# Attention in a streaming encoder step: late gates in another order, and the output weights fetched in three groups

## The chip, the cores and the metric

The kernel runs on one core of a Trainium2 chip. The core has a matrix engine (TensorE, PE in the profile), a vector engine (DVE), a scalar engine (ACT), a general engine (POOL) and a sync engine (SP). SP computes nothing; it issues the DMA transfers of its own queue, in the order of its program. The metric is device time in microseconds for one execution of the whole program, as the median of several runs.

## The reference

The program is one inference step of a two-layer encoder on 2048 prompt tokens and 32 sampled tokens, 1024 wide. Layer A is a gated DeltaNet. Layer B, with which the change is concerned, is attention over a sliding window of whole chunks of 64 tokens, with 16 query heads on 4 shared key and value heads, a learned sink per head, a gate, an output projection and a layer norm:

```python
def swa_layer(x, k, v, pos, cached, w_in, sinks, w_out, ln_g, ln_b):
    b, l, _ = x.shape
    proj = x @ w_in
    q = rope_partial(proj[..., :B_QW].reshape(b, l, B_Q_HEADS, B_HD), pos) * (B_HD ** -0.5)
    q = q.reshape(b, l, B_KV_HEADS, B_GROUP, B_HD)
    z = proj[..., B_QW:]
    sk = sinks.reshape(B_KV_HEADS, B_GROUP)
    o = cached_attention(q, k, v, sk) if cached else banded_attention(q, k, v, sk)
    out = (o * jax.nn.silu(z)) @ w_out
    return layer_norm(DN_ALPHA * x + out, ln_g, ln_b)
```

`z` is the gate. `x @ w_in` for the columns of `z` is what the text calls the gates; `@ w_out` is the output product.

## The kernel before

Every product with a weight matrix is made from two halves of each float32 factor, a high part and the rest, in three matmuls: high by high, high by low, low by high (`project`, L79 to L81). A weight slab of 128 columns is fetched whole (512 KB, `fetch_weights`, L48, into the one buffer `w_raw`), cast to its high part on ACT and subtracted on another engine (`split_fetched`, L55 and L56). The pool of slabs has two buffers, so two slabs can be used at a time.

The tokens stand in five blocks of 416 (0 to 4). The class `P2` keeps all five blocks in on-chip memory as high and low parts: blocks 0 and 1 in the pool `p2_resr` on the right side of the memory, blocks 2, 3 and 4 on the left. It makes keys, values, queries and gates. There are eight gate slabs, 0 to 7. Slabs 0 to 3 are done for all blocks; slabs 4 to 7 at first for blocks 2, 3 and 4 only. What is left, four slabs by blocks 0 and 1, are the eight late gates. They are run within attention, as work for TensorE while the first softmaxes are made. Each gate is 24 matmuls, a tanh and a scaling on ACT (L1428, L1429, tiles `zs` and `za`), one operation on DVE (L1430) and a store to `s_bz` on SP (L1431). The pool of `za` has three buffers, so the fourth gate from here writes into the buffer whose store must have landed.

`Attention.run` writes out the order of the work by hand for all five engines. It takes the chunks 14 to 31 and then 0 to 13, in steps: scores, largest value, exponentials, shares, transposes (L1713), values (L1731), and the gating of the result. Between the first steps `fill(n)` lets the generator `gates` go on by n half gates: two gates before the first exponentials, one each in the three places after them, and one in each of the steps 0, 1 and 2. The gates' sums use the two banks `oa` and `ob` in turn, the same two that hold the values' result of each step.

From step 3 on, each step has one half of an output product (512 of 1024 columns, eight weights, each with three matmuls, L1146 to L1148). The output weights lie split in memory as `s_wob`; weight k takes 1 MB with both parts. `weights` (L1468) fetches weights 0 to 2 in the course of the third late gate. `load_late` (L1484) fetches 3 to 7: its pool needs the memory of `P2`'s right side, which is free when the last late gate is done, in step 2. Behind the first two of these five SP asks for the first row tile `r` (L1547), and behind the rest for the layer norm's tables and for the keys and values of the chunks 0 to 11.

Two lines show how the late gates are placed before the change:

```python
for j, i in enumerate((6, 7, 4, 5)):
    for b in (0, 1):
```

The slabs 6 and 7 are still in the two buffers; 4 and 5 are fetched and split a second time, 4 in the course of the third gate and 5 in the course of the fifth.

Of the kernel before, what the change touches and what calls it, by code (L numbers as in the profile page):

```python
# [11 lines left out]
F32 = mybir.dt.float32  # L12
# [9 lines left out]
D = 1024  # L22
# [70 lines left out]
def drain(gen):  # L93
    for _ in gen:
        pass


class P1:
# [243 lines left out]
    def split(self):  # L342
        self.cast()
        self.subtract()
# [947 lines left out]
class P2:  # L1292
# [3 lines left out]
    def __init__(self, tc, right, spare, I, O, T):  # L1296
        self.tc, self.nc, self.I, self.O, self.T = tc, tc.nc, I, O, T
        self.resr = new_pool(tc, right, "p2_resr", 1, side="right")
        self.wp = new_pool(tc, right, "p2_w", 2, side="right")
        self.wk = new_pool(tc, right, "p2_wk", 3, side="right")  # L1300
        self.stg = new_pool(tc, spare, "p2_stg", 2, side="right")
        self.ppr = new_pool(tc, spare, "p2_psr", 2, PSUM, side="right")
        self.ppl = None
        self.turn = 0
        self.x = {}
        self.w = {}

    def load_right(self):
        for b in (0, 1):
            self.load(b, self.resr)  # L1310

    def open_left(self, left):
        self.resl = new_pool(self.tc, left, "p2_resl", 1, side="left")
# [120 lines left out]
class Attention:  # L1434


    EARLY = 3

    def __init__(self, tc, left, I, O, T, G):
        self.tc, self.nc, self.I, self.O, self.T, self.G = tc, tc.nc, I, O, T, G  # L1440
        nc, V = tc.nc, tc.nc.vector
        L = "left"
        self.one = one = new_pool(tc, left, "t_one", 1, side=L)
        self.two = new_pool(tc, left, "t_two", 3, side=L)
        self.thr = new_pool(tc, left, "t_thr", 4, side=L)
# [12 lines left out]
        self.sinks = one.tile([128, 12, 2], F32, tag="twice", name="twice")  # L1458
        V.tensor_copy(self.sinks[:], raw[:].unsqueeze(2).to_broadcast([128, 12, 2]))
        self.S = [self.ps_s.tile([128, 2, 2, 256], F32, tag=f"S{p}", name="S") for p in range(2)]  # L1460
        self.held = {}
# [9 lines left out]
    def load_early(self):  # L1471
        self.w = self.weights(self.first, 0, self.EARLY)

    def open_right(self, right):
        tc, I = self.tc, self.I
# [2 lines left out]
        self.otwo = new_pool(tc, right, "u_two", 2, side=R)  # L1478

    def load_late(self):  # L1480
        w = self.oone.tile([128, 2, KC - self.EARLY, D], F32R, tag="wo", name="wo")
        for k in range(self.EARLY, KC):
            x = w[:, :, k - self.EARLY]
            self.nc.sync.dma_start(x.bitcast(F32), self.T["wob"][:, k].rearrange("a p d -> p a d"))  # L1484
            self.w.append(x)
            if k == self.EARLY + 1:
                yield
# [456 lines left out]
def program(tc, I, O, T, G):  # L1944
# [99 lines left out]
    att = Attention(tc, left, I, O, T, G)  # L2044

    def gates(raw):
        for j, i in enumerate((6, 7, 4, 5)):
            for b in (0, 1):
                g = p2.gate(i, (b,), lambda: att.out_bank(b))
                next(g)  # L2050
                next(g)
                if b == 0:
                    if j in (1, 2):
                        p2.w[3 + j] = split_fetched(nc, p2.wp, raw, nc.vector)
                    if j == 1:
                        raw = fetch_weights(nc, p2.wp, I["b_w_in"][13])
                    if j == 1:
                        att.load_keys(18, 32)
                        att.load_values(18, 32)
                        att.load_early()  # L2060
                yield
                drain(g)
                yield

    def opened():
        right.close()
# [164 lines left out]
```

## Time and profile before

| what | value |
|---|---|
| median of 3 runs | 2122.08 us (2119.59 to 2124.72) |
| the profiled execution's own time | 2119.22 us |
| its span | 2117.1 us |
| TensorE busy | 2078.8 us, 98% |
| VectorE, ScalarE, GpSimd busy | 62%, 43%, 39% |
| mean DMA rate | 145 GB/s |
| late gates and first steps of attention | about 1719 to 1784 us |
| first output product | from 1783.76 us |

The span is the time from the first to the last instruction of the program in one profiled execution; all times within it count from its start. TensorE is busy nearly all the time, so time is lost where it waits, and where it is granted half its clock. The views used below are the list of waits (who waited for whom: total, times, longest), the chain of waits, the timeline of an engine (start, length, engine, line, what, and in brackets the idle time before and what ended it) and windows (busy time of PE, its weight loads, DVE, ACT and POOL with their counts, then the granted clock, the mean share of the DMA engines, and GB/s).

### The profile page before, as it was taken

The page shows a single profiled execution, that of the slowest core. Times are in us where ns is not written, and L with a number is a line of the kernel's source. Part 1 is how long each engine was busy: PE and PEld are TensorE (multiplying, and loading weights), DVE is VectorE, ACT ScalarE, POOL GpSimd, SP SyncE. Part 2 cuts the span into 40 slices and gives each one's busy share as a digit, 9 for nine tenths or more (in the row PEclk, how much of TensorE's full clock was granted, in tenths as well). Part 3 has the DMA queues.
Part 4 walks back from the last instruction along what each step waited for, and adds up shares of the span by engine and source line. Part 5 has one row for each costly group of instructions (what it writes and reads, how often), then busy time and mean ns, then how long its engine had stood idle before and what let it go on. Part 6 is the DMA issues. An engine that isn't in the chain of part 4 may idle for free.

```text
span 2117.1 us, 37205 instructions
## 1 busy us (share of the span) xinstructions
PE 2078.8 (98%) x14062; PEld 1912.6 (90%) x14062; DVE 1306.6 (62%) x2449; ACT 901.1 (43%) x2263; POOL 834.6 (39%) x1179
## 2 busy tenths in 40 slices
PE   8999999999999999999999999999999998999998
PEld 6999999999999999999888888999999996777775
DVE  4676666666557688889978885225543223566665
ACT  4444444445622377677752212322111233455552
POOL 1422222222122187878830302136443103566765
PEclk9999999999999999999999999999999998999999
DMA  5222332346664545556846764455222257534321
GB/s 206 67 65 82 111 111 92 96 128 207 197 197 153 178 157 180 163 171 210 278 159 204 240 194 131 135 196 202 82 72 70 75 143 259 137 100 120 100 72 65
DMA packets 263636, 307.26 MB, mean 145 GB/s; under 512 B 71409, under 2 KB 194609, under 8 KB 263185
## 3 DMA queue, kind: packets, MB, share of 16 engines
q1 hardware_dynamic: 252208, 281.40, 42.7%
q10 hardware_dynamic: 11248, 23.48, 3.4%
q8 instruction: 111, 1.82, 0.4%
q14 instruction: 69, 0.56, 0.1%
HBM read 188.58 MB, written 116.60 MB: 144 GB/s over the span
## 4 chain that ended last, share of the span: by engine, by line
PE 91%; POOL 3%; DMA 2%; DVE 2%; ACT 1%; issue 1%; SPq 1%; ACTq 0%; POOLq 0%; DVEq 0%
PE ps L79 17%; PE ps L81 17%; PE ps L80 17%; PE ot L1146 3%; PE po L1146 3%; PE po L1148 3%; PE po L1147 3%; PE ot L1148 3%; PE ot L1147 3%; PE S L1698 2%; PE ot L1731 2%; PE tr L1713 2%; POOL tm L729 1%; POOL Tt L731 1%; PE g L695 1%; PE gq L831 1%
## 5 line engine op out<-in xcount | busy, mean ns | idle before, releaser
L79 PE MATMUL ps<-act_hi,w_hi 128*128 128x416 f32 x1936 | 683.3, 354 | 1.4 <-ACT act_hi L70 1.4
L81 PE MATMUL ps<-act_hi,w_lo 128*128 128x416 f32 x1936 | 681.3, 352 | 0.9 <-POOL w_lo L56 0.9
L80 PE MATMUL ps<-act_lo,w_hi 128*128 128x416 f32 x1936 | 678.2, 350 | 0.4 <-DVE act_lo L71 0.4
L79 PEld LDWEIGHTS ps<-act_hi,w_hi 128*128 128x128 f32 x1936 | 364.1, 188 | 6.6 <-ACT act_hi L70 2.1
L80 PEld LDWEIGHTS ps<-act_lo,w_hi 128*128 128x128 f32 x1936 | 363.8, 188 | 4.8 <-DVE act_lo L71 0.8
L81 PEld LDWEIGHTS ps<-act_hi,w_lo 128*128 128x128 f32 x1936 | 363.4, 188 | 4.7 <-POOL w_lo L56 1.3
L56 POOL TENSOR_TENSOR w_lo<-w_raw,w_hi 128x1024 fp32r<-128x1024 f32 x44 | 117.1, 2661 | 470.3 <-ACT w_hi L55 443.1
L209 DVE SCALAR_TENSOR_TENSOR y<-R,convw,y 128x2083 f32<-128x2083 f32 x72 | 182.7, 2538 | 62.8 <-ACT y L206 46.9
L1537 POOL TENSOR_TENSOR P<-e,sm 128x384 f32<-128x384 f32 (+2 forms) x128 | 101.2, 812 | 181.7 <-DVE sm L1527 175.7
L729 POOL TENSOR_TENSOR tm<-L,Tt 128x60 f32<-128x60 f32 (+19 forms) x365 | 133.2, 365 | 78.8 <-issue 39.9
L731 POOL TENSOR_TENSOR Tt<-Tt,tm 128x60 f32<-128x60 f32 (+19 forms) x365 | 140.8, 386 | 28.6
L1523 ACT ACTIVATE e<-S,nm 128x193 f32<-128x193 f32 (+2 forms) x260 | 104.8, 416 | 95.9 <-DVE nm L1518 58.2
L1146 PE MATMUL ot<-wo,g_hi 128*128 128x512 f32 x256 | 104.6, 409 | 6.1 <-DMA wo<-s_wob 6.1
L305 ACT COPY R<-ps 128x416 f32<-128x416 f32 (+1 forms) x144 | 60.3, 442 | 108.3 <-PE ps L81 95.7
L1146 PE MATMUL po<-wo_hi,g_hi 128*128 128x512 f32 x256 | 103.3, 404 | 0.2 <-ACT g_hi L1188 0.2
L1345 POOL TENSOR_TENSOR rs<-rs,sin 128x416 f32<-128x416 f32 x50 | 70.7, 1414 | 80.3 <-DVE rs L1344 73.5
L1148 PE MATMUL ot<-wo,g_lo 128*128 128x512 f32 x256 | 101.2, 395 | 0.0
L1147 PE MATMUL ot<-wo,g_hi 128*128 128x512 f32 x256 | 101.1, 395 | 0.0
L1148 PE MATMUL po<-wo_hi,g_lo 128*128 128x512 f32 x256 | 100.2, 392 | 0.5 <-DVE g_lo L1189 0.5
L1430 DVE SCALAR_TENSOR_TENSOR za<-zs,za 128x416 f32<-128x416 f32 x40 | 31.7, 796 | 111.3 <-ACT za L1429 111.1
L1147 PE MATMUL po<-wo_lo,g_hi 128*128 128x512 f32 x256 | 99.9, 390 | 0.0
L55 ACT CAST w_hi<-w_raw 128x1024 fp32r<-128x1024 f32 x46 | 48.3, 1051 | 93.5 <-PE ps L80 74.4
(299 smaller groups left out, 3917.9 us busy)
## 6 DMA issues: line engine op xcount, KB each, us to landing
w_raw<-in_w_in SPq DMA_DIRECT2D x40, 512.0 KB
w_raw<-in_b_w_in SPq DMA_DIRECT2D x18, 512.0 KB
k<-s_k SPq DMA_DIRECT2D x17, 512.0 KB
E<-s_E SPq DMA_DIRECT2D x17, 512.0 KB
s_bz<-za SPq DMA_DIRECT2D x40, 208.0 KB
s_bq<-ra SPq DMA_DIRECT2D x40, 208.0 KB
s_q<-y SPq DMA_DIRECT2D x8, 1024.0 KB
s_wo<-wo_parts SPq DMA_DIRECT2D x16, 512.0 KB
```

Source lines behind the costliest of these rows:

```text
L56: sub.tensor_tensor(out=lo[:], in0=raw[:], in1=hi[:], op=ALU.subtract)
L79: nc.tensor.matmul(ps, hi[:, k, :], xh[:, k, :], start=(k == 0), stop=False)
L80: nc.tensor.matmul(ps, hi[:, k, :], xl[:, k, :], start=False, stop=False)
L81: nc.tensor.matmul(ps, lo[:, k, :], xh[:, k, :], start=False, stop=(k == KC - 1))
L209: nc.vector.scalar_tensor_tensor(out=y[:], in0=R[:, j:j + W], scalar=self.convw[:, i, j:j + 1], in1=y[:], op0=ALU.mult, op1=ALU.add)
L729: P.tensor_tensor(out=tm[:n, i0 - k:, :w], in0=L[:n, i0:, j:j + 1].to_broadcast(sh), in1=Tt[:n, j:j + 1, :w].to_broadcast(sh), op=ALU.mult)
L731: P.tensor_tensor(out=Tt[:n, i0:, :w], in0=Tt[:n, i0:, :w], in1=tm[:n, i0 - k:, :w], op=ALU.subtract)
L1146: nc.tensor.matmul(ps[:n], ghi[:, k, :n], hi, start=a, stop=False)
L1147: nc.tensor.matmul(ps[:n], ghi[:, k, :n], lo, start=False, stop=False)
L1148: nc.tensor.matmul(ps[:n], glo[:, k, :n], hi, start=False, stop=z)
L1523: self.nc.scalar.activation(x.e[:, h, u, :x.n], x.S[:, h, u, :], AF.Exp, bias=x.nm[:, h, u:u + 1], scale=1.0, accum_out=x.sm[:, h, u:u + 1])
L1537: self.nc.gpsimd.tensor_tensor(out=x.P[:, u, :nj * 128].rearrange("r (j h k) -> r j h k", h=2, k=64), in0=x.e[:, :, u, :n].rearrange("r h ...
```

## The change

The eight late gates get another order, written as pairs of slab and block: (6,0), (7,0), (7,1), (4,0), (5,0), (4,1), (5,1), (6,1). Block 0 is used for the last time by the fifth of them. It now has a pool of its own, `p2_resf`, which is closed in the sixth gate, and the memory goes to a new pool on the left side for the output weights 3, 4 and 5, asked for at that point. Weights 0, 1 and 2 are asked for one in the course of the fourth gate and two in the fifth, where all three were asked for in the third. `load_late` keeps 6 and 7. Since slab 6 is used first and last, it is fetched and split once more: three slabs are split in the late gates (4 in the second gate, 5 ahead of the fourth, 6 in the seventh) where there were two.

```diff
+        self.front = ExitStack()
+        self.resf = new_pool(tc, self.front, "p2_resf", 1, side="right")
...
         for b in (0, 1):
-            self.load(b, self.resr)
+            self.load(b, (self.resf, self.resr)[b])
...
     EARLY = 3
+    LATE = 6
...
     def weights(self, pool, a, z):
         w = pool.tile([128, 2, z - a, D], F32R, tag="wo", name="wo")
+        self.w += [w[:, :, k] for k in range(z - a)]
         for k in range(a, z):
             self.nc.sync.dma_start(w[:, :, k - a].bitcast(F32), self.T["wob"][:, k].rearrange("a p d -> p a d"))
-        return [w[:, :, k] for k in range(z - a)]
+            yield
...
+    def middle_weights(self, left):
+        return self.weights(new_pool(self.tc, left, "t_wo2", 1, side="left"), self.EARLY, self.LATE)
...
     def load_late(self):
...
+        drain(self.weights(self.oone, self.LATE, KC))
+        yield
         self.tabs = ln_tables(self.nc.sync, self.oone, self.I["b_ln_g"], self.I["b_ln_b"])
...
+        for m, (i, b) in enumerate(((6, 0), (7, 0), (7, 1), (4, 0), (5, 0), (4, 1), (5, 1), (6, 1))):
+            if m == 3:
+                split(5)
+            g = p2.gate(i, (b,), lambda: att.out_bank(m % 2))
+            next(g)
+            next(g)
+            if m == 1:
+                split(4)
+            elif m == 2:
+                att.load_keys(18, 32)
+                att.load_values(18, 32)
+                early = att.early_weights()
+            elif m == 3:
+                next(early)
+            elif m == 4:
+                drain(early)
+            elif m == 5:
+                p2.front.close()
+                drain(att.middle_weights(left))
+            elif m == 6:
+                split(6)
+            yield
+            drain(g)
+            if m in (1, 4):
+                raw = fetch_weights(nc, p2.wp, I["b_w_in"][8 + (5, 6)[m // 4]])
+            yield
```

The first place is SP's queue during the late gates, from the values of chunks 18 to 31 (`vd`) to the row tile (of the after, stores and loads for later steps are left out at the dots). `wo` are output weights of 1 MB each, `s_bz<-za` the gates' stores, `w_raw` a gate slab, `qs` and `zs` queries and gates of coming steps, `r` the row tile. Before:

```order
L1497 DMA vd<-s_bv 64x14x128 x2
L1468 DMA wo<-s_wob 128x2x1024 x3
L1431 DMA s_bz<-za 128x416 x3
L1676 DMA qs<-s_bq 128x8x64 x2
L1681 DMA zs<-s_bz 128x8x128
L1431 DMA s_bz<-za 128x416
L1676 DMA qs<-s_bq 128x8x64 x2
L1431 DMA s_bz<-za 128x416
L1681 DMA zs<-s_bz 128x8x128
L1484 DMA wo<-s_wob 128x2x1024 x2
L1547 DMA r<-s_h 128x1024
L1484 DMA wo<-s_wob 128x2x1024 x3
```

The same stretch of SP's queue in the changed kernel:

```order
L1433 DMA s_bz<-za 128x416
L1473 DMA wo<-s_wob 128x2x1024
L1433 DMA s_bz<-za 128x416
L1473 DMA wo<-s_wob 128x2x1024 x2
L1433 DMA s_bz<-za 128x416
L48 DMA w_raw<-in_b_w_in 128x1024
L1679 DMA qs<-s_bq 128x8x64 x2
L1684 DMA zs<-s_bz 128x8x128
L1473 DMA wo<-s_wob 128x2x1024 x3
L1433 DMA s_bz<-za 128x416
...
L1473 DMA wo<-s_wob 128x2x1024 x2
L1550 DMA r<-s_h 128x1024
```

The three early weights stand between the gates' stores now, three more stand behind the first queries and gates, and two are left ahead of the row tile.

The second place is ACT's queue from the first late gate's end to the first copy of a transpose (`pt`). `zs` and `za` are a gate's tanh and scaling, `e` the exponentials of one softmax, `w_hi` the cast of a gate slab. Before:

```order
L1428 ACTIVATE zs<-ot 128x416
L1429 ACTIVATE za<-ot 128x416
L1523 ACTIVATE e,sm<-S,nm 128x193 x4
L55 CAST w_hi<-w_raw 128x1024
L1428 ACTIVATE zs<-ot 128x416
L1429 ACTIVATE za<-ot 128x416
L1523 ACTIVATE e,sm<-S,nm 128x193 x4
L1428 ACTIVATE zs<-ot 128x416
L1429 ACTIVATE za<-ot 128x416
L1523 ACTIVATE e,sm<-S,nm 128x193 x4
L1719 COPY pt<-tr 128x384
L55 CAST w_hi<-w_raw 128x1024
```

In the changed kernel:

```order
L55 CAST w_hi<-w_raw 128x1024
L1430 ACTIVATE zs<-ot 128x416
L1431 ACTIVATE za<-ot 128x416
L1526 ACTIVATE e,sm<-S,nm 128x193 x4
L1430 ACTIVATE zs<-ot 128x416
L1431 ACTIVATE za<-ot 128x416
L1526 ACTIVATE e,sm<-S,nm 128x193 x4
L55 CAST w_hi<-w_raw 128x1024
L1430 ACTIVATE zs<-ot 128x416
L1431 ACTIVATE za<-ot 128x416
L1526 ACTIVATE e,sm<-S,nm 128x193 x4
L1722 COPY pt<-tr 128x384
```

The cast of slab 4 moved from behind the first exponentials to the place ahead of the second gate's tanh, and the cast of slab 5 from behind the fourth gate and the first copy to the place ahead of that gate's tanh. The subtractions on DVE moved in the same way. POOL's rows stand as they stood.

More of the change, by code (lines that the diff above doesn't have):

```diff
@@ L1466, in weights, with early_weights @@
         w = pool.tile([128, 2, z - a, D], F32R, tag="wo", name="wo")
+        self.w += [w[:, :, k] for k in range(z - a)]
         for k in range(a, z):
             self.nc.sync.dma_start(w[:, :, k - a].bitcast(F32), self.T["wob"][:, k].rearrange("a p d -> p a d"))
-        return [w[:, :, k] for k in range(z - a)]
-    def load_early(self):
-        self.w = self.weights(self.first, 0, self.EARLY)
+            yield
+    def early_weights(self):
+        return self.weights(self.first, 0, self.EARLY)
+    def middle_weights(self, left):
+        return self.weights(new_pool(self.tc, left, "t_wo2", 1, side="left"), self.EARLY, self.LATE)
     def open_right(self, right):
@@ L1480, in load_late @@
     def load_late(self):
[L1481 to L1487, printed above, removed]
+        drain(self.weights(self.oone, self.LATE, KC))
+        yield
         self.tabs = ln_tables(self.nc.sync, self.oone, self.I["b_ln_g"], self.I["b_ln_b"])
@@ L2046, in gates, with split @@
     def gates(raw):
[L2047 to L2063, printed above, removed]
+        def split(j):
+            p2.w[j] = split_fetched(nc, p2.wp, raw, nc.vector)
+        for m, (i, b) in enumerate(((6, 0), (7, 0), (7, 1), (4, 0), (5, 0), (4, 1), (5, 1), (6, 1))):
[24 more added lines that the diff above has]
+            yield
     def opened():
```

1 line of the change is left out of this document (added).

## The prediction

> **What bounds the kernel now.** I read the page, the list of waits, the timelines of TensorE (PE) and of the sync queue (SP), and windows for clock and DMA. What the change can win is idle or slow TensorE in its own stage, out of a span of 2117.1 us.
>
> ```profile
> span 2117.1 us, 37205 instructions
> ...
> L1146 PE MATMUL ot<-wo,g_hi 128*128 128x512 f32 x256 | 104.6, 409 | 6.1 <-DMA wo<-s_wob 6.1
> ```
>
> The second row is the output product of attention: its 6.1 us of idle time are waits for the output weights. The waits between 1690 and 1830 us add another, and the chain of waits says how old it is:
>
> ```profile
> ACT za L1429 <- DMA s_bz<-za: 2.8, 1, 2.8
> ...
> PE ot L1731 <- ACT za L1429: 1.8, 1, 1.8
> ```
>
> ```profile
> 1745.27 13.19 DMA s_bz<-za
> ```
>
> A gate's result leaves through one of three za buffers. The store issued at 1745.27 lands 13.19 us later, behind 3 MB of weights; ScalarE (ACT) waits 2.8 us for its buffer and TensorE 1.8 us for ACT. What both stalls cost is read from TensorE's timeline (start, length, what, idle before):
>
> ```profile
> 1740.98 0.43 PE L79 MATMUL ot<-act_hi,w_hi 128*128 128x416 f32 x1
> ...
> 1756.60 0.64 PE L1731 MATMUL ot<-pt,vd 64*64 64x256 f32 x2
> ...
> 1764.28 0.43 PE L79 MATMUL ot<-act_hi,w_hi 128*128 128x416 f32 x1
> ...
> 1770.49 1.82 PE L1731 MATMUL ot<-pt,vd 64*64 64x256 f32 x24
> ...
> 1773.72 0.43 PE L79 MATMUL ot<-act_hi,w_hi 128*128 128x416 f32 x1
> ...
> 1783.76 0.48 PE L1146 MATMUL ot<-wo,g_hi 128*128 128x512 f32 x1
> ...
> 1788.37 0.50 PE L1146 MATMUL ot<-wo,g_hi 128*128 128x512 f32 x1 [1.42 <-DMA wo<-s_wob]
> ...
> 1794.76 0.80 PE L1146 MATMUL ot<-wo,g_hi 128*128 128x512 f32 x1 [0.91 <-DMA wo<-s_wob]
> ...
> 1797.32 0.80 PE L1146 MATMUL ot<-wo,g_hi 128*128 128x512 f32 x1 [0.91 <-DMA wo<-s_wob]
> ...
> 1801.77 1.53 PE L1731 MATMUL ot<-pt,vd 64*64 64x256 f32 x24
> ...
> 1804.70 0.48 PE L1146 MATMUL ot<-wo,g_hi 128*128 128x512 f32 x1
> ...
> 1810.32 0.82 PE L1713 MATMUL tr<-ident,P 128*128 128x128 f32 x6
> 1811.06 0.92 PE L1698 MATMUL S<-kT,qs 64*128 64x192 f32 x8
> 1811.91 0.45 PE L1731 MATMUL ot<-pt,vd 64*64 64x256 f32 x4
> ```
>
> Stall A: from the values to the next gate 1756.60 to 1764.28, 7.68 us; the same work one step later, 1770.49 to 1773.72, takes 3.23. A costs 4.45. Stall B: from the first output product to the values of the next step 1783.76 to 1801.77, 18.01 us; one step later 1804.70 to 1811.91, 7.21. B costs 10.80. Both exceed the idle time because the clock falls as well (last three figures of a row: granted clock, DMA share, GB/s):
>
> ```profile
> 1757.43:1760.84 3.41, 1.71 (x20) 0.92 (x22) 1.81 (x4) 0.89 (x2) 0.96 (x2) 1.00 0.81 186
> 1760.84:1764.25 3.41, 3.41 (x22) 2.28 (x15) 0.94 (x3) 1.87 (x9) 0.66 (x1) 0.50 1.15 303
> 1784.73:1788.14 3.41, 2.22 (x10) 1.46 (x8) 1.00 (x3) 1.72 (x8) 2.03 (x3) 1.00 1.02 419
> 1788.14:1791.56 3.42, 0.97 (x3) 0.48 (x3) 0.00 (x0) 0.00 (x0) 1.21 (x2) 1.00 1.02 411
> ```
>
> TensorE busy for 1.71 of 3.41 us is followed by a stretch at 0.50; busy for 2.22 it is followed by 1.00. A gap of 1.2 us costs itself, one of 1.7 us also half of 3.41, that is 1.7 us.
>
> **The change, part by part.** I call the eight late gates G0 to G7. TensorE's work is the same 24 matmuls a gate, in another order.
>
> *Weights 3 to 7 of the output product.* Three of the five that B waited for are now asked for after G4, two where all five stood. The late request:
>
> ```profile
> 1780.55 0.93 SPq L1484 DMA_DIRECT2D wo<-s_wob  x2
> ```
>
> Two of 1 MB go out at 1780.55, call it T0; the second is there when the wait at 1788.37 ends, T0+7.8. In the changed kernel these two are the last ones, numbers 6 and 7. The product starts at T0+3.2 and takes (1810.32 - 1804.70)/8 = 0.70 us for each of eight weights, so number 7 is wanted at T0+8.1: just in time. The row of activations r comes 1.3 us later (half of the 2.56 us a megabyte takes, 1794.76 to 1797.32) and is wanted when the product ends, at T0+8.8, with 1.6 us of transposes and scores (1810.32 to 1811.91) before TensorE needs its bank again. B goes, 10.80, if the queue is empty at T0. Between the stages it was idle:
>
> ```profile
> 1765.00:1770.00 5.00, 5.00 (x32) 4.75 (x32) 1.07 (x3) 2.63 (x11) 1.62 (x2) 1.00 0.02 5
> ...
> 1775.00:1780.00 5.00, 5.00 (x35) 4.53 (x34) 1.01 (x3) 3.19 (x11) 1.62 (x2) 1.00 0.01 1
> ```
>
> That is 10 us; the change puts 3 MB and 0.5 MB of gate weights in front, 9.0 us at 2.56. It fits with 1 us to spare. What goes back on B if the cover is gone: 2.56 us for each megabyte still queued, and half clock beyond 1.2 us of gap.
>
> *Early weights 0 to 2*, now between the gates' stores. The store that took 13.19 us stands in front of them, so A goes, 4.45; za's next wait is for a store one megabyte later, with more than a gate's time in hand. The three weights land about 1 us later (two more stores of 208 KB ahead of them) and are wanted at T0+3.2: nothing.
>
> *SP's new wait.* The first middle weight waits for TensorE to leave the first block (end of G4). Behind it on SP stand G5's store, the next queries, G6's store and the next gates' loads; none is read before T0. The loads ahead of the new wait held SP long in the run before:
>
> ```profile
> 1747.76 8.21 SPq L1676 DMA_DIRECT2D qs<-s_bq  x2
> ```
>
> That holds SP until 1756, when the run before was through with its sixth gate too (the values at 1756.60 follow it), so G4 is done even 4.1 us later: nothing, and 1 us at most if SP came earlier, since only the queue's slack pays.
>
> *Gate weights w4 and w5, needed earlier.* This is the cost. Before, w4 was used by the fifth gate and w5 by the seventh; now by G3 and G4, one and two gates sooner, while w5's fetch stands where it stood:
>
> ```profile
> 1735.68 1.34 SPq L48 DMA_DIRECT2D w_raw<-in_b_w_in  x1
> ```
>
> Its landing has no row, since nobody waited. I bound it by bytes. Issued since 1722.7, up to and with it:
>
> ```profile
> qs<-s_bq SPq DMA_DIRECT2D x4, 256.0 KB
> w_raw<-in_b_w_in SPq DMA_DIRECT2D x2, 512.0 KB
> zs<-s_bz SPq DMA_DIRECT2D x2, 512.0 KB
> s_bz<-za SPq DMA_DIRECT2D x2, 208.0 KB
> kT<-s_bk SPq DMA_DIRECT2D x1, 384.0 KB
> vd<-s_bv SPq DMA_DIRECT2D x2, 192.0 KB
> ```
>
> ```profile
> 1722.70:1740.00 17.30, 17.30 (x100) 15.86 (x101) 4.99 (x8) 7.70 (x26) 1.62 (x2) 1.00 1.10 255
> ```
>
> 4256 KB are 4.36 MB; 255 GB/s for 17.3 us are 4.41 MB. It lands at 1740.0 at the earliest, and as the 16 engines end apart I take 1741.5 as the late end. Then come the cast and the subtraction:
>
> ```profile
> 1744.20 1.08 ACT L55 CAST w_hi<-w_raw 128x1024 fp32r<-128x1024 f32 x1
> ```
>
> ```profile
> 1733.61 1.23 DVE L56 TENSOR_TENSOR w_lo<-w_raw,w_hi 128x1024 fp32r<-128x1024 f32 x1 [2.79 <-ACT w_hi L55]
> ```
>
> They end at 1742.3 to 1743.8. G4 starts where the fifth gate started, 1740.98, and gets 0.4 us of work done with the high part alone. Stall C is 0.9 to 2.4 us. I take 2.4, since a transfer counts only when its slowest engine is done, and 1.7 for the clock, since a window with 2.4 us of gap is emptier than the one that halved it above: 4.1. For w4 the queue holds 1408 KB (kT, two qs, itself), a third of that, 5.7 us at 255 GB/s, so it lands between 1728.4 and about 1730; its cast now heads ACT's queue ahead of G1's tanh and the first exponentials, which come 3 us later, and the first transposes (just before 1740.98) still find their input about 1 us early: nothing, and up to 1 us if not.
>
> The Trainium skill (TensorE: Matmul & The Clock Gate, "Why this matters for your kernels") asks for no gaps above about 3 us between bursts of matmuls. By that, C would not touch the clock, and the sum below would be 1.7 us lower. The rows above, in which 1.7 us of gap in one window was enough, speak against it, and I keep 1.7.
>
> *A third split (w6 again for G7).* A cast of 1.08 and a subtraction of 1.23 us more. Their cover is the wait of ACT and VectorE (DVE) for G6's matmuls:
>
> ```profile
> 1769.09 0.52 ACT L1428 ACTIVATE zs<-ot 128x416 f32<-128x416 f32 x1 [1.29 <-PE ot L81]
> ```
>
> ```profile
> 1770.05 0.59 DVE L1430 SCALAR_TENSOR_TENSOR za<-zs,za 128x416 f32<-128x416 f32 x1 [3.98 <-ACT za L1429]
> ```
>
> 1.08 goes into 1.29: nothing, or about 1 us if the cast comes late, since the values wait for this gate's bank.
>
> *Block 0 in a pool of its own.* No work is added. It makes the planner move two fetches of gate weights behind stores, and three products behind four small steps, near 1111 to 1128 us, where TensorE is full:
>
> ```profile
> 1125.00:1130.00 5.00, 5.00 (x24) 4.14 (x23) 4.78 (x10) 1.05 (x1) 0.00 (x0) 1.00 0.92 284
> ```
>
> I take nothing, and 1 us either way since DVE has 0.22 us free there.
>
> **Sum.** -4.45 (A) - 10.80 (B) + 4.1 (C) = -11.15 us. The profiled execution took 2119.22, its span and 2.1 us around it: 2108.1. The median shown, 2122.08, is 2.9 above that execution and would give 2110.9. I forecast 2109.5, between the two.
>
> **Rivals.**
> 1. C is small: the raw w5 lands at 1740 and the clock holds. -15.25 + 0.9 = -14.3, 2105 to 2108. For it: the bytes; against it: the slowest engine. 0.19.
> 2. B goes only in part: the queue is not empty at T0, since small packets move slower than the weights (255 against 411 GB/s in the rows). With 2 MB left, 5.1 us come back and half clock for one window: -11.15 + 6.8 = -4.3, 2115 to 2118. Against it: 10 us idle for 9.0. 0.17; about half of it lies inside 0.2%.
> 3. Slower: the memory of block 0 comes free late. If SP's new wait ended only near T0 (say with G6, because the new tile also covers bytes still in use), all that stands behind it goes out there: 3 MB, three stores of 208 KB, 512 KB of queries and 512 KB of gates ahead of the last 2 MB. Before, the last weight landed at 1797.3, T0+16.7, behind 5 MB and r; now 1.1 MB more, T0+19.5, and r after it, 4.1 us in all. B is then 14.9 with A gone and C paid: +3.8, and 1.3 for w6's fetch in the same queue: +5.1, 2124 to 2127. It decides from a wait that ends 5 us before T0 or later. Against it: only one TensorE event is waited for, and the pool closes after G4. 0.06.
> 4. Nothing measurable: C cascades through ACT's queue (exponentials behind the cast of w5) until it eats A and most of B, 10 us more than I take: 2118 to 2121. No row shows such a chain, since the next transposes wait for TensorE's own gate. 0.03.
>
> **How the numbers follow.** My forecast has 0.55, from C's and the 1 us bounds 2106.5 to 2113. The range 2104 to 2119 takes in rivals 1 and 2 and leaves out 3 and 4 and the tails. 0.2%, about what a measurement of this kernel can tell from no change, is 4.2 us: faster means under 2117.8. Faster 0.55 + 0.19 + half of rival 2, rounded to 0.83; same, 0.11, from the rest of 2 and from 4; slower 0.06.
>
> **What would show it.** Right: no wait of TensorE on wo and none of za on s_bz; first product to next values near 7.2 us; one wait of G4's matmuls on ACT's w_hi and DVE's w_lo, some 2.4 us, and 0.50 clock behind it; the queue idle just before the last two weights go out. Wrong: waits on weights 6 and 7, or SP standing at the middle weights until G6.

## The result, and the profile after

The changed kernel takes 2112.1 us, the median of six runs (2111.02 to 2116.91), beside 2121.76 us for the kernel before (2119.59 to 2124.72, six runs): a ratio of 0.9964, with a 95% interval of 0.9952 to 0.9975 (the two medians by themselves give 0.9954, inside the interval). Run once more, in a later batch, it took 2111.1 us (2109.43 to 2115.35) beside 2120.0: 0.9958, 0.9944 to 0.9973. The profiled execution took 2112.2 us, its span 2110.4.

The page's row of the output product has no idle time left, where 6.1 us stood:

```profile
span 2110.4 us, 37218 instructions
...
L1146 PE MATMUL ot<-wo,g_hi 128*128 128x512 f32 x256 | 103.6, 405 | 0.0
```

The list of waits between 1690 and 1830 us names neither wo nor s_bz any more. What TensorE waits for now is the gate weights, stall C; for the row tile r only DVE waits (columns: total, times, longest, us):

```profile
ACT w_hi L55 <- DMA w_raw<-in_b_w_in: 6.3, 2, 5.5
...
DVE r L1154 <- DMA r<-s_h: 2.4, 1, 2.4
...
PE ot L79 <- ACT w_hi L55: 1.2, 1, 1.2
...
PE ot L81 <- DVE w_lo L56: 0.6, 1, 0.6
```

The timeline of TensorE after the change (start, length, what, idle before):

```profile
1730.89 0.92 PE L1701 MATMUL S<-kT,qs 64*128 64x192 f32 x8
1731.74 0.46 PE L79 MATMUL ot<-act_hi,w_hi 128*128 128x416 f32 x1
...
1745.01 0.46 PE L79 MATMUL ot<-act_hi,w_hi 128*128 128x416 f32 x1 [1.20 <-ACT w_hi L55]
...
1746.27 0.71 PE L81 MATMUL ot<-act_hi,w_lo 128*128 128x416 f32 x1 [0.61 <-DVE w_lo L56]
...
1756.83 0.43 PE L79 MATMUL ot<-act_hi,w_hi 128*128 128x416 f32 x1
...
1763.05 0.45 PE L1734 MATMUL ot<-pt,vd 64*64 64x256 f32 x4
...
1766.28 0.43 PE L79 MATMUL ot<-act_hi,w_hi 128*128 128x416 f32 x1
...
1785.76 0.48 PE L1146 MATMUL ot<-wo,g_hi 128*128 128x512 f32 x1
...
1793.16 0.66 PE L1734 MATMUL ot<-pt,vd 64*64 64x256 f32 x8
...
1796.10 0.48 PE L1146 MATMUL ot<-wo,g_hi 128*128 128x512 f32 x1
...
1803.37 0.88 PE L1734 MATMUL ot<-pt,vd 64*64 64x256 f32 x12
```

From the values to the next gate it takes 1763.05 to 1766.28, 3.23 us, so A is gone; from the first output product to the next values 1785.76 to 1793.16, 7.40 us in place of 18.01, so B is gone. C shows at 1745 and 1746 us, and half clock follows it; just ahead of T0 (1782.54 here) the transfers run out (last three figures of a row: granted clock, DMA share, GB/s):

```profile
1742.82:1746.23 3.41, 1.64 (x12) 0.94 (x8) 1.24 (x2) 2.18 (x5) 0.00 (x0) 1.00 1.10 297
1746.23:1749.65 3.42, 3.38 (x10) 3.23 (x11) 1.89 (x4) 1.90 (x9) 1.62 (x2) 0.50 1.19 193
...
1775.00:1780.00 5.00, 5.00 (x31) 4.87 (x30) 1.63 (x4) 2.96 (x14) 1.62 (x2) 1.00 0.82 211
1780.00:1782.50 2.50, 2.50 (x21) 1.69 (x19) 1.00 (x3) 1.96 (x4) 0.15 (x1) 1.00 0.05 15
```

The sync queue's timeline, with the three middle weights and, at T0, the last two:

```profile
1755.80 6.59 SPq L1684 DMA_DIRECT2D zs<-s_bz  x1
1762.48 1.85 SPq L1473 DMA_DIRECT2D wo<-s_wob  x3
...
1782.54 0.93 SPq L1473 DMA_DIRECT2D wo<-s_wob  x2
```

From here on I cut each profiled execution at two places of TensorE's timeline: the first scores (1730.89 above) and the second values after the first output product (1803.37 above). Between them lies what I call the opening, 72.5 us; behind them the rest, 307.0 us to the end of the span. The kernel before has 83.6 (1728.30 to 1811.91) and 305.2.

| kernel | opening, us | rest, us | half clock in the opening behind | ratio to the kernel before, 95% |
|---|---|---|---|---|
| before | 83.6 | 305.2 | A and B | 1 |
| changed | 72.5 | 307.0 | C | 0.9964 (0.9952 to 0.9975) |
| changed, again | 72.6 | 307.0 | C | 0.9958 (0.9944 to 0.9973) |
| five weights late again | 84.1 | 305.4 | C and B | 1.0016 (1.0007 to 1.0024) |
| early weights at once | 71.4 | 307.0 | none | 0.9971 (0.9961 to 0.9981) |
| w5's gate later | 68.6 | 307.0 | none | 0.9955 (0.9943 to 0.9967) |
| w5's gate later, early weights at once | 73.3 | 307.0 | A | single run |
| weights 32 bytes up | 71.3 | 305.2 | none | 0.9954 (0.9942 to 0.9966) |
| w5's gate later, 32 bytes up | 68.5 | 305.2 | none | 0.9948 (0.9932 to 0.9964) |
| w5's gate later, 96 bytes up | 68.9 | 306.4 | none | 0.9940 (0.9923 to 0.9957) |
| w5's gate later, 64 bytes up | 69.2 | 307.2 | none | 0.9951 (0.9932 to 0.9970) |
| high and low part side by side | 70.9 | 307.0 | none | single run |
| before, front pool alone | 81.9 | 305.5 | B | 1.0010 (0.9997 to 1.0023) |
| before, weights 96 bytes up | 81.8 | 304.6 | B | 0.9997 (0.9985 to 1.0009) |

Of the six executions with 96 bytes, one took 2553.17 us at a granted clock of 0.75 and is left out of the ratio. The medians of the kernel before differ by up to 3.4 us between batches (2118.40 to 2121.76), so a term of 1 or 2 us is read from these stages and their waits, not from the medians. Each stage comes from one profiled execution.

### The profile page after: what moved, and what is told of

Its sections match the earlier page's. It is cut to its first block, busy times and chain, and to the rows that moved or that the text cites. A ratio compares the mean times of both kernels' runs of the same rounds, so it can differ in the third digit from the quotient of the medians.

```text
span 2110.4 us, 37218 instructions
## 1 busy us (share of the span) xinstructions
PE 2076.7 (98%) x14062; PEld 1911.9 (91%) x14062; DVE 1309.2 (62%) x2450; ACT 901.9 (43%) x2264; POOL 833.9 (40%) x1179
## 4 chain that ended last, share of the span: by engine, by line
PE 92%; DVE 3%; DMA 2%; POOL 1%; ACT 1%; issue 1%; SPq 0%; ACTq 0%; DVEq 0%; POOLq 0%
PE ps L79 17%; PE ps L81 17%; PE ps L80 17%; PE ot L1146 3%; PE ot L1147 3%; PE ot L1148 3%; PE po L1146 3%; PE po L1148 3%; PE po L1147 3%; PE S L1701 2%; PE ot L1734 2%; PE tr L1716 2%; PE g L695 1%; PE gq L831 1%; PE ks L846 1%; PE sp L846 1%
```

## The experiments

### Is B the gain, and do A and C cancel?

The changed kernel with all five weights late again; gates, early weights and pool as changed:

```diff
-        drain(self.weights(self.oone, self.LATE, KC))
+        late = self.weights(self.oone, self.EARLY, KC)
+        next(late)
+        next(late)
         yield
+        drain(late)
...
-                drain(att.middle_weights(left))
```

> The changed kernel with weights 3 to 7 asked for late again, two ahead of the row tile and three behind it, as in the kernel before; gate order, three splits and spread early weights stay. Theory: the gain is stall B alone, 10.6 us by the profile after, while A (4.45 won) and C (3.9 paid) cancel; the products lose the 0.05 us they each take longer (31 of them, 1.6 us). So B returns: first product to next values 16 to 18 us, 2112.1 + 10.6 - 1.6 = about 2121 us. Rival (the gates' order and the spread stores made the gain): 2112 to 2115 us.

It took 2122.11 us (2117.88 to 2125.8) beside 2118.4: 1.0016, no gain at all. TensorE's timeline shows B as it was:

```profile
1787.22 0.48 PE L1146 MATMUL ot<-wo,g_hi 128*128 128x512 f32 x1
...
1791.88 0.50 PE L1146 MATMUL ot<-wo,g_hi 128*128 128x512 f32 x1 [1.47 <-DMA wo<-s_wob]
1795.73 0.62 PE L1146 MATMUL ot<-wo,g_hi 128*128 128x512 f32 x1 [2.88 <-DMA wo<-s_wob]
...
1805.28 1.08 PE L1737 MATMUL ot<-pt,vd 64*64 64x256 f32 x8
```

From 1787.22 to 1805.28 are 18.06 us. The waits show no za behind s_bz, and C is there (1.7 and 0.6 us of TensorE's waits). So all of the gain hangs on the three weights that go out earlier, and what the new order of gates wins by A it pays for C.

### Does spreading the early weights take A away?

First on the changed kernel, with weights 0 to 2 asked for in the third gate all at once, as before:

```diff
-                early = att.early_weights()
-            elif m == 3:
-                next(early)
-            elif m == 4:
-                drain(early)
+                drain(att.early_weights())
```

> The changed kernel with weights 0 to 2 asked for in one go in the third gate again, ahead of that gate's store. Theory that spreading them is what ended stall A: ACT waits for s_bz again and 4.45 us come back, 2116.5 us. Rival: the wait for w5 delays the sixth gate by 3.9 us, and the store, 5.1 us later than now (two more weights ahead), lands at about 1757 us after the start of the profile's span, before that gate's za is written at 1761: no wait, 2112 us within 1.

A did not come back: no wait on s_bz, 2111.96 us (2110.22 to 2117.74), opening 71.4. My reason had named the spreading, so this spoke against it. But a store still stands behind 3 MB, three at a time:

```profile
1747.02 0.64 SPq L1473 DMA_DIRECT2D wo<-s_wob  x1
1747.76 4.96 SPq L1433 DMA_DIRECT2D s_bz<-za  x3
```

The first of the three is complete at 1760.54, 12.8 us after its issue (13.19 in the kernel before), and ACT takes its buffer again at 1760.62. It was in time by 0.1 us, in an execution in which C had held back every gate by 2.8 us. So the next run asks for the weights at once where C is gone, on the kernel with w5's gate one place later (below):

```diff
-                early = att.early_weights()
-            elif m == 3:
-                next(early)
-            elif m == 4:
-                drain(early)
+                drain(att.early_weights())
+            elif m == 4:
                 split(5)
```

> The kernel with w5's gate one place later (where stall C is gone), and output weights 0 to 2 asked for all three in the third gate, as in the kernel before. With C in place such a request cost nothing: the store behind it landed at 1760.54 us and its buffer was wanted at 1760.62, so C's 2.9 us of delay may have been the cover. Theory (without C the buffer is wanted about 2.3 us earlier, so stall A comes back in part, and spreading the request is what keeps it away): ACT waits 1.5 to 2.5 us for za on s_bz, TensorE 0.5 to 1.7 us behind it; 69.3 to 70.3 us from the first score to the second values in place of 68.6, 1.7 more if a half clock follows. Rival (the order of the gates removes A whatever the request): no such wait, 68.6 us.

A is back. The waits around the opening:

```profile
ACT za L1431 <- DMA s_bz<-za: 2.6, 1, 2.6
...
PE ot L1734 <- ACT za L1431: 1.6, 1, 1.6
```

The chain of waits has the store again, with the time it took to land:

```profile
1749.43 12.56 DMA s_bz<-za
```

And in the windows half clock follows:

```profile
1760.93:1764.34 3.41, 1.72 (x21) 0.89 (x22) 1.77 (x4) 0.89 (x2) 0.92 (x2) 1.00 1.12 316
1764.34:1767.75 3.41, 3.41 (x21) 2.23 (x16) 0.98 (x3) 1.79 (x9) 0.69 (x1) 0.50 0.84 230
```

The opening is 73.3 us against 68.6 without this edit. Of these 4.7 us, 4.25 lie between the values and the next gate (1760.34 to 1767.82, 7.48 in place of 3.23), which is A, half clock included. The other 0.4 us fall at the values one step earlier; the runs with 96 and 64 bytes below, which have no such edit, lose 0.3 and 0.6 there too. So spreading the request does take A away. In the changed kernel it is only a second cover, since C's delay hides A too.

### C alone: the gate of w5 one place later

```diff
-        for m, (i, b) in enumerate(((6, 0), (7, 0), (7, 1), (4, 0), (5, 0), (4, 1), (5, 1), (6, 1))):
-            if m == 3:
-                split(5)
+        for m, (i, b) in enumerate(((6, 0), (7, 0), (7, 1), (4, 0), (4, 1), (5, 0), (5, 1), (6, 1))):
...
             elif m == 4:
                 drain(early)
-            elif m == 5:
+                split(5)
+            elif m == 6:
                 p2.front.close()
                 drain(att.middle_weights(left))
-            elif m == 6:
                 split(6)
```

> Order (6,0), (7,0), (7,1), (4,0), (4,1), (5,0), (5,1), (6,1): slab 5 is used one gate later, its split stands in the fifth gate, and the memory of block 0 goes over one gate later. Theory: C is the landing of w5's raw slab, so no wait on w_hi or w_lo remains and 3.9 us go, 2108.2 us, if the queue keeps up; in the profile after it was busy until 1782.4 and the last two weights went out at 1782.5, so with 3.9 us less time before it weight 7 and the row tile may come some 2.4 us late, 2110.6 us. Rival (C is made by the order of casts and exponentials on ACT, not by the landing): a wait of 2 us or more moves to the sixth gate, 2112 us.

The split of slab 5 and the release of block 0's memory move back with the gate. TensorE waits for no gate weights any more, and the late gates start at an even pace:

```profile
1731.82 0.46 PE L79 MATMUL ot<-act_hi,w_hi 128*128 128x416 f32 x1
...
1743.65 0.43 PE L79 MATMUL ot<-act_hi,w_hi 128*128 128x416 f32 x1
...
1753.03 0.43 PE L79 MATMUL ot<-act_hi,w_hi 128*128 128x416 f32 x1
...
1762.48 0.43 PE L79 MATMUL ot<-act_hi,w_hi 128*128 128x416 f32 x1
```

From the first late gate after the first scores to the fourth it takes 1731.82 to 1753.03, 21.2 us, where the changed kernel takes 1731.74 to 1756.83, 25.1: C costs 3.9 us. The three middle weights now go out two us later, and the first product still reaches the next values in 7.4 us. The margin is smaller, though: transfers ran at a share of 1.05 up to 1778.00, 0.75 us ahead of the last two weights (1778.75), where the changed kernel had 2.5 us with a share of 0.05; part of that slack was C's delay. The run took 2109.14 us (2107.17 to 2111.19), 0.9955: not resolved against the changed kernel by the medians, but the stage is 3.9 us shorter.

### When the half clock follows a gap

C did not cost the same everywhere. With the same two waits in TensorE's row (1.2 to 1.7 and 0.6 us), half clock followed in the changed kernel, in its repeat and with five weights late; it did not with the early weights at once, the weights 32 bytes up or the parts side by side, and there the same stage took 24.0, 24.0 and 23.5 us in place of 25.1 to 25.6. The windows below tell why. They are laid so that one begins where a half clock of the same execution begins, and follow each other by 3.413 us. The changed kernel again:

```profile
1740.39:1743.80 3.41, 1.67 (x12) 0.94 (x8) 0.94 (x1) 1.95 (x4) 0.00 (x0) 1.00 0.99 293
1743.80:1747.22 3.42, 3.08 (x9) 2.95 (x10) 2.19 (x5) 1.60 (x9) 1.62 (x2) 0.50 1.19 205
```

The early weights at once:

```profile
1742.06:1745.47 3.41, 1.79 (x16) 1.23 (x12) 0.41 (x1) 2.17 (x7) 0.00 (x0) 1.00 1.01 313
1745.47:1748.88 3.41, 2.79 (x15) 2.51 (x14) 2.71 (x5) 1.45 (x6) 1.62 (x2) 1.00 1.18 198
```

The weights 32 bytes up:

```profile
1740.64:1744.06 3.42, 1.75 (x15) 1.13 (x12) 0.47 (x1) 1.88 (x5) 0.00 (x0) 1.00 1.08 324
1744.06:1747.47 3.41, 2.79 (x16) 2.59 (x15) 2.65 (x5) 1.44 (x7) 1.62 (x2) 1.00 1.20 187
```

The first busy figure is TensorE's: 1.64, 1.67 and 1.72 us (the run with A, above) of 3.41 are followed by 0.50, 1.75 and 1.79 by 1.00. In these rows the switch lies at about half of a window. Where the windows begin is different in each execution: where C's second wait of 0.6 us falls into the next window, as in the last two, the first wait alone does not empty half of one. So a gap of 1.2 to 2.3 us costs 1.7 us more, or not, depending on where a window happens to begin. The same holds for A: the two later kernels with A in place had no half clock behind it, and there values to next gate took 5.2 (front pool alone) and 6.3 us (before, 96 bytes up) in place of 7.68. The Trainium skill (TensorE: Matmul & The Clock Gate, "What's actually happening") says that the window runs free of the kernel and lasts 3413 ns, and the runs agree: a half clock behind A or C lasts 3.41 us and begins at a different place of the work each time. It has the clock fall after an idle window, and here a half-idle one was enough.

The busy figure sorts only the windows of attention's opening. Further ahead, among smaller matmuls, it does not. In the changed kernel TensorE was busy throughout a window, and half clock followed:

```profile
735.88:739.30 3.42, 3.42 (x30) 3.04 (x30) 1.88 (x4) 2.57 (x8) 1.90 (x7) 1.00 0.45 147
739.30:742.71 3.41, 3.41 (x18) 2.82 (x16) 1.07 (x4) 3.21 (x13) 2.65 (x9) 0.50 0.51 156
```

In the kernel before, 1.58 us busy of the window at 1016.73 were followed by 1.00; in the run with A back, 1.80 us of the one at 1027.06 by 0.50. So half of a window is no rule for the whole program, and what the clock goes by stays open.

### What the output product lost: 1.8 us behind the opening

The sum of the prediction ended at the opening. Behind it the changed kernel lost 1.8 us (307.0 against 305.2), in steps whose order of work the change does not touch. The step from values to values shows it; the kernel before:

```profile
1852.53 1.53 PE L1731 MATMUL ot<-pt,vd 64*64 64x256 f32 x24
...
1862.69 1.53 PE L1731 MATMUL ot<-pt,vd 64*64 64x256 f32 x24
```

The changed kernel:

```profile
1854.40 1.53 PE L1734 MATMUL ot<-pt,vd 64*64 64x256 f32 x24
...
1864.61 1.53 PE L1734 MATMUL ot<-pt,vd 64*64 64x256 f32 x24
```

10.16 us have become 10.21. From the second product to the last, 29 steps, it is 292.86 us in place of 291.33, so 1.5 of the 1.8 us lie there; the other 0.3 fall between the start of the last product and the end, which takes 21.07 us in the kernel before, 21.41 in the changed one and 21.36 in the kernel before with the front pool alone, whose output weights lie where they lay. The product's own time I read from its weight loads (PEld): its 24 loads take 5.24 us from first to last start, 5.20 before, as medians over the products of an execution. In the kernel before, the first nine matmuls are about 234 ns apart and those with the late weights settle to 227 ns; now nearly all run at 232 to 234. What differs for them is where their operands lie in on-chip memory: weights 0 to 2 at byte 114688 of a partition in both kernels, 3 to 7 at 180192 before, now 3 to 5 at 139264 and 6 and 7 at 204768. The other factor, g_hi, moved too, from 163296 to 187872 for one of its buffers, by a multiple of 128. I took the rest of the address by 64 for the cause, and moved weights 0 to 5 by 32 bytes:

```diff
+        if a == 0:
+            pool.tile([128, 8], F32, tag="pad", name="pad")
         w = pool.tile([128, 2, z - a, D], F32R, tag="wo", name="wo")
```

> The changed kernel with output weights 0 to 5 placed 32 bytes higher in on-chip memory (at 32 instead of 0 modulo 64); nothing else moves. In the profile before, products over weights at 32 modulo 64 settle at 227 ns a matmul and those over weights at 0 modulo 64 run at 233 to 234. Theory (alignment): a product falls from 5.24 to about 5.1 us, 31 of them win 4.2 us, 2108 us. Rival (the place, left or right of the memory, or the size of the tile decides): 5.24 us stay, 2112 us.

```profile
1851.04 1.53 PE L1736 MATMUL ot<-pt,vd 64*64 64x256 f32 x24
...
1861.18 1.53 PE L1736 MATMUL ot<-pt,vd 64*64 64x256 f32 x24
```

A step takes 10.14 us, a product 5.18, the rest 305.2 us: the 1.8 us are back, but not the 4.2 that I expected: the spacing fell from 233 to 230 ns on average, not to 227. So the place of the weights alone moves a product's time, and the rule was not right. Two more sizes of the same pad, both with w5's gate later, and one of them on the kernel before:

> The kernel with w5's gate one place later, and the output weights 0 to 5 moved up by 96 bytes in place of 32, so that all of their addresses leave the same rest by 128 (96) as weights 6 and 7 and the products' other operand, g. Theory 1 (what counts is whether the two operands of a product leave the same rest by 128; O1's do, and its products run at 227 ns): 227 ns throughout, a product of 24 takes about 5.11 us in place of 5.24, 31 of them -4.0 us, what follows the second values 303 us; total about 2105. Theory 2 (only the rest by 64 counts, which the 32 bytes changed already): as with 32 bytes, 5.18 us, 305.2 us behind the second values; total 2107. Theory 3 (placement is not it): 5.24 us, 307.0, total 2109. The opening of attention stays at 68.6 us in all three.

> As the run beside it, with 64 bytes in place of 96: weights 0 to 5 leave the rest 64 by 128, and 0 by 64 as in the changed kernel. Theory 1 (same rest by 128 as g): not the same, so slow, about 5.24 us for a product of 24 matmuls and 307 us behind the second values. Theory 2 (rest by 64): 5.24 us as well. Rival (any shift helps, as neighbouring tiles no longer collide): 5.18 us or less, 305 us. Total 2109 by the theories, 2107 by the rival.

> The kernel before with nothing changed but the place of its output weights 0 to 2, 96 bytes further up, where they leave the same rest by 128 as weights 3 to 7 and g. In the kernel before, the first nine matmuls of each product come 234 ns apart and settle to 227 ns with the later weights. Theory 1: all at 227 ns, a product takes 5.11 us in place of 5.19, 31 of them -2.5 us; what follows the second values takes 302.7 us in place of 305.2; ratio 0.9988. Theory 2 (rest by 64): at least the same gain. Theory 3 (the spacing has another cause, such as what DVE or ACT do beside the first third of a product): 5.19 us, 305.2 us, ratio 1.000.

96 bytes up, the step is 10.18 us:

```profile
1850.06 1.53 PE L1736 MATMUL ot<-pt,vd 64*64 64x256 f32 x24
...
1860.24 1.53 PE L1736 MATMUL ot<-pt,vd 64*64 64x256 f32 x24
```

A product takes 5.22 us at 96 bytes, 5.23 to 5.24 at 64, and 5.17 in the kernel before moved by 96 bytes (5.20 unmoved; rest 304.6 us). Both rules fall: by 64, 32 and 96 should be alike; by 128, 96 should be the fastest. The times of these runs were 2107.73 us with 96 bytes (the median of all six), 2109.94 with 64 and 2119.38 for the kernel before moved. A last guess was the distance between the high and the low part of a weight:

```diff
-        w = pool.tile([128, 2, z - a, D], F32R, tag="wo", name="wo")
-        self.w += [w[:, :, k] for k in range(z - a)]
+        w = pool.tile([128, z - a, 2, D], F32R, tag="wo", name="wo")
+        self.w += [w[:, k] for k in range(z - a)]
...
-            self.nc.sync.dma_start(w[:, :, k - a].bitcast(F32), self.T["wob"][:, k].rearrange("a p d -> p a d"))
+            self.nc.sync.dma_start(w[:, k - a].bitcast(F32), self.T["wob"][:, k].rearrange("a p d -> p a d"))
```

> The changed kernel with another layout of the output weights alone: high and low part of one weight side by side (4096 bytes apart) in place of all high parts ahead of all low parts (12288 bytes apart for weights 0 to 5, 8192 for 6 and 7). In the kernel before, products settled to 227 ns with weights 3 to 7 (20480 apart) and in O1 (32768 apart), and ran at 232 to 234 ns with 12288 and 8192. Theory (the distance between the two parts sets the spacing): the time of a product moves off 5.24 us by at least 0.05 us, either way. Rival (distance has no part in it): 5.23 to 5.25 us. Attention's opening stays at 71.3 to 72.5 us.

One run took 2113.87 us; a product takes 5.24 us as before this edit, with the same sequence of spacings. The distance is not it. What is shown: the median product repeats to the nanosecond between runs on different chips for one placement (5.239 us in every run with the changed kernel's places, 5.181 in both with 32 bytes up), and a shift of the weights alone moves it. How much of the step from 5.20 to 5.24 us is due to the weights and how much to g_hi was not tried, and which property of the place decides stays open.

### The front pool: not nothing

O1 is the output product of layer A, long ahead of attention. In every changed kernel TensorE lost 1.15 to 1.7 us against the kernel before on the stretch that this one works off between 1125 and 1140 us, where O1 stands. The edit alone, on the kernel before:

```diff
+        self.front = ExitStack()
+        self.resf = new_pool(tc, self.front, "p2_resf", 1, side="right")
...
-            self.load(b, self.resr)
+            self.load(b, (self.resf, self.resr)[b])
...
     def opened():
+        p2.front.close()
         right.close()
```

> The kernel before with one part of the change alone: block 0 in a pool of its own (which is closed only where the other one is). In every changed kernel so far TensorE loses 1.1 to 1.9 us between 1118 and 1140 us against the kernel before, and shows there a wait of an O1 product on r of DVE (0.8 us) that the kernel before has not. Theory (the pool shifts the gates' weights by 26 KB into memory that is freed later, and so re-orders fetches and DVE's steps): the wait of 0.8 us stands here too, the same stage is 1.0 to 1.6 us longer, attention from the first score to the second values after the first output product stays at 83.6 us and what follows at 305.2: about +1.2 us, ratio 1.0006. Rival (it is scatter, or comes with the late gates' order): no such wait, the stage as before, ratio 1.000.

The wait of the changed kernel stands in this one too. The changed kernel, then the front pool alone:

```profile
1135.57 0.47 PE L1146 MATMUL po<-wo_hi,g_hi 128*128 128x512 f32 x1 [0.79 <-DVE r L1154]
```

```profile
1133.83 0.47 PE L1146 MATMUL po<-wo_hi,g_hi 128*128 128x512 f32 x1 [0.79 <-DVE r L1154]
```

The kernel before has no such wait, and the stretch is 1.4 us longer here, 1.15 in the changed kernel. Three steps of DVE (L929) come late for TensorE. They stood ahead of four small steps and stand behind them now, but that order is not what costs: DVE is idle behind the small ones until the fetch of its input z lands. The kernel before, then the front pool alone:

```profile
1125.08 1.49 DVE L929 TENSOR_TENSOR z<-otr,z 128x128 f32<-128x128 f32 x3 [2.01 <-DMA z<-s_z]
```

```profile
1126.72 1.49 DVE L929 TENSOR_TENSOR z<-otr,z 128x128 f32<-128x128 f32 x3 [2.11 <-DMA z<-s_z]
```

SP asks for z at 1122.72 us in the one and 1122.63 in the other, and with the front pool it is there 1.64 us later. A fetch of 512 KB of raw gate weights, which went out at 1111.79 before, now goes out at 1120.98, just ahead of z. That it delays z is likely, but was not tried by itself. Nor does the loss stay whole: where the kernel before is at 1140 us this run is 1.49 us behind it, and the repeat of the changed kernel 1.68; at 1500 us they are 0.50 and 0.20 behind. In between, TensorE waits 1.4 us for act_hi in the kernel before, 0.6 in its copy with the weights 96 bytes up and 0.2 in this run, so executions differ there by as much. 2123.13 us (2117.79 to 2126.36) beside 2119.35, 1.0010, cannot tell 1.4 us from nothing; the wait can. The gates' raw weights moved from byte 151520 to 178144 with this edit, which is what I hold to be behind the new order of fetches; that part was not tried by itself either.

### The two edits that paid, together, and the changed kernel beside them

The order of w5's gate later and the pad of 32 bytes, as above:

> The two edits that paid, together: w5's gate one place later, and weights 0 to 5 up by 32 bytes. If they add, attention takes 68.6 to 68.9 us from the first score to the second values after the first output product (as with the later gate alone), a product of 24 matmuls 5.18 us and what follows 305.2 us (as with the 32 bytes alone): 2105.5 to 2107.5, ratio about 0.994. If the spacing of a product hangs on more than this place (96 bytes gave 5.22, so it may not be stable), it is 5.2 to 5.24 us, 306 to 307 us, 2109.

> The changed kernel itself once more, beside the others on the same chip. Ratio to the kernel before 0.9952 to 0.9975, as measured before. In its profile: 5.24 us for a product of 24, the wait of 0.8 us at 1132 us, C's two waits of TensorE (1.2 to 1.7 and 0.6 us); behind them half clock for 3.41 us where TensorE was busy for less than 1.72 us of one clock window, and full clock where the gap is split between two windows: 72.5 us by the first, 71.3 by the second from the first score to the second values.

They add: opening 68.5, rest 305.2, no half clock in the opening. It took 2109.13 us (2105.88 to 2111.9), 0.9948, beside 2111.1 and 0.9958 for the changed kernel on the same chip. By the stages it is 5.9 us ahead (68.53 and 305.18 against 72.63 and 307.00); the medians show 2.0, and their intervals overlap, so as a time the gain over the changed kernel is not resolved. The spans differ less than the stages because of what lies ahead: its first scores came at 1731.78 us, the repeat's at 1728.50, by windows of half clock at 740 and 1023 us that the second had not.

## Why the prediction was right, and what it missed

The forecast was 2109.5 us in 2104 to 2119, faster with 0.83; it took 2112.1 us. By its own steps:

- **B goes, 10.80 us.** Right: 10.6 (18.01 to 7.40), and the run with five weights late shows that the gain hangs on it. The two stated signs held: no wait on wo, and the queue nearly idle in the 2.5 us ahead of T0 (DMA share 0.05). About 2 us were left where I had counted 1, and part of them only because C delayed T0; with C gone, half a microsecond was left and B stayed away.
- **A goes, 4.45 us, by the spread of the early weights.** Right in cause and size: 4.25 us where it came back. It left out that C's own delay would have hidden A, and that 1.7 of the 4.45 are a half clock that two other executions of A did not have.
- **C, 4.1 us.** The wait is where it was placed, 1.8 us of TensorE's own time and 3.9 in all with the half clock; 2.3 to 2.8 without. The cast of w5 started when its slab landed, 13.0 us behind the first scores (1743.92), near the late end of the 11.7 to 13.2 us that the bytes and the slowest engine had given. Of rival 1, the part that the clock holds came true in three profiled executions of six; that C is small (0.9 us) did not. The weighing of the Trainium skill's rule on gaps above about 3 us (TensorE: Matmul & The Clock Gate, "Why this matters for your kernels") came out against the rule, but a flat 1.7 us was not right either: it is paid or not, by where the window begins.
- **SP's new wait: nothing; a third split: nothing.** Right: SP issued the three middle weights at 1762.48, behind 6.59 us of its own at zs, and no wait of TensorE follows G6's or G7's weights.
- **Block 0 in its own pool: nothing, 1 us either way.** Mis-sized: 1.15 us lost in the changed kernel, 1.4 alone, at the place that was named; of the 1.4, 0.5 us are left where attention begins.
- **What the sum did not contain:** the output products of the whole rest. The step that failed is that "TensorE's work is the same 24 matmuls a gate, in another order" was taken for the output products too; they are the same matmuls, but their operands lie elsewhere, and that costs 1.5 of the 1.8 us by which the rest is longer.

With these sizes: -4.45 - 10.6 + 3.9 + 1.8 + 1.15 = -8.2 us, where -11.15 was forecast; without the pool's 1.15, which may not last, it is -9.35. The two ratios say -0.0036 and -0.0042 of 2120, -7.6 and -8.9 us, and the first pair of medians -9.7. So the sum promised 1.5 to 3.5 us more than was won, and it is the width of the range, 15 us, that took this in. Ahead of attention the rest of a profile's difference (2.6 us later at the first scores in the changed kernel) is the 1.15 and single windows of half clock, at 739 us in this execution, which other executions of the same program have elsewhere or not at all.

Rivals 2, 3 and 4 did not show: the queue was empty at T0, SP's wait did not end near T0, and C did not run on into the exponentials' chain.

## What to carry to other kernels

Free a buffer earlier and the request that B waited for goes out earlier; look then at what the freed place costs upstream, since here a gate that came too early for its weights took back 3.9 us, nearly the 4.45 that the end of stall A had given. Weigh a gap by how much of one clock window it can empty, and give it a range, with the half clock and without, since its place in the window is not yours to choose. When a tile moves to another address, time the same matmuls on it again: they need not run as before.

## What was not expected of the hardware

- Behind stalls A and C the granted clock fell for one window of 3.41 us when TensorE had been busy for less than about half of the window before: 1.64 to 1.72 us did it, 1.75 and 1.79 did not. Among smaller matmuls ahead of it this does not hold: half clock followed a window that was busy throughout (at 735.88 in the changed kernel) and one with 1.80 us (at 1027.06 in the run with A back), and did not follow one with 1.58 us (at 1016.73 in the kernel before).
- The spacing of matmuls of 128x512 moves between 227 and 234 ns with the place of their operands in on-chip memory, and a shift of the weights alone is enough. The weight loads of a product of 24 take 5.239 us with the changed kernel's places, 5.181 with the weights 32 bytes further up, 5.22 with 96, 5.23 to 5.24 with 64; the median repeats to the nanosecond between runs.
